# Layer A's output projection as seven half-size block products, with x added by accumulating DMAs and the roundings on ScalarE

## The chip, the cores and the metric

The kernel runs on one core of one Trainium2 chip. The metric is the device time of one execution in microseconds (us). TensorE does the matrix products, VectorE (DVE in the profile) and ScalarE (ACT) work elementwise, GpSimd (POOL) here rounds operands and issues a few DMAs, and SyncE (SP) issues most DMAs. All of them run beside each other and wait for one another through semaphores; each engine works through its own list of instructions in order.

## What is computed

Two layers of a streaming encoder over 1024 frames of width 1024. Layer A (an mLSTM mixer and a pooling mixer) ends with the step that is changed here:

```python
# ya, yb: (1, 1024 tokens, 1024) each;  w_out: (2048, 1024)
return x + jnp.concatenate([ya, yb], axis=-1) @ w_out
```

Layer C (latent attention) begins with `u = rms_norm(x, norm_g) @ w_in` on that result and adds its own output to it at the end, so the result of layer A is needed twice: normalised and transposed at once (`x1h`, `x1l`), and as it is at the end of the kernel (kept in DRAM as `x1_d`).

## The kernel before, in words

All products are float32 products made of three passes in the fast format float32r. Each operand is cut into a rounded part `hi` and the rest `lo = src - hi` (`split`, L156 rounds on GpSimd or L158 on ScalarE, L161 subtracts on VectorE), and `mm3` (L176 to L178) issues hi\*hi, hi\*lo and lo\*hi into the same PSUM bank. A source tile of 128 x 1024 float32 (512 KB) thus costs a DMA, a rounding, a subtraction, and then serves many matmuls of 128 x 128 by 128 x 512.

Up to the projection, layer A's heads are worked through from head 3 to head 0. Their outputs go feature-major to DRAM (`y_d`, 2048 features by 1024 tokens); the last four stores are those of head 0's `zm_pieces` (L336), each behind a block of 24 matmuls (tile `fp_ps`), a SiLU on ScalarE (L415) and a product on VectorE (L417).

The projection then runs over two token halves (512 tokens each), in each over two halves of the output columns, and in each over eight chunks of 256 features. A chunk has 24 matmuls: four token tiles, two row blocks, three passes, into four PSUM banks (tile `o_ps`). So there are 2 x 2 x 8 x 24 = 768 of them. `load_y` reads and splits a chunk of y once per token half (16 tiles, `yh` and `yl`); `load_wo` reads and splits a chunk of the weights for each of the four blocks (32 tiles, `w_hi` and `w_lo`). x itself is loaded into the eight tiles `x1t`, and L875 adds the PSUM banks to it. When four tiles of 128 tokens are complete they are stored to `x1_d` and normalised (`norm_stats`: squares on ScalarE L823, the power on GpSimd L213, the scaling on VectorE L827); `x1_turn` transposes them on TensorE (L834, tile `nt_ps`) into `x1h` and `x1l`. Next come layer C's input products (`u_tiles`, tile `u_ps`), whose first four tiles need the first token half only.

The order in which each engine meets its instructions is settled when the program is built: a scheduler places them by a timeline of its own, within what tile pools (a fixed number of buffers for each tag) and data allow. DMAs that are marked to keep program order, such as the new loads, stay in it on SP.

Of the kernel before, what the change touches and what calls it, by code (L numbers as in the profile page):

```python
# [88 lines left out]
def _hybrid(ctx, tc, nc, ins, consts, out, dbg):  # L89
# [699 lines left out]
    ys = {}

    def load_y(half, n):
        kp = order[n]
        yp = yps[0 if n < EARLY else 1]
        yh = yp.tile([P, 2, HALF], F32R, name="yh", tag=f"yh{n}", bufs=1)
        yl = yp.tile([P, 2, HALF], F32R, name="yl", tag=f"yl{n}", bufs=1)
        wload([P, 2, HALF], y_d[kp * 256:(kp + 1) * 256, half * HALF:(half + 1) * HALF].rearrange("(k p) t -> p k t", p=P), into=(yh, yl))
        ys[half, n] = (yh, yl)
# [6 lines left out]
    load_y(0, 0)
    wo = [load_wo(0, 0)]
    for n in range(1, EARLY):
        load_y(0, n)
# [29 lines left out]
    halves = []  # L837

    def x1_turn(half):
        hs_ = slice(half * HALF, (half + 1) * HALF)  # L840
        norm_turn([t[:] for t in halves[half]], "c_norm_g", lambda k: x1h[:, k, hs_], lambda k: x1l[:, k, hs_])

    for half in range(2):
        if half == 1:
# [4 lines left out]
            x1l = x1p.tile([P, KD, S], F32R, name="x1l")
        x1t = []  # L850
        halves.append(x1t)
        for ch in range(2):
            cs = slice(ch * HALF, (ch + 1) * HALF)
            pss = []
            for j in range(4):
                ps = pmm.tile([P, 512], F32, name="o_ps", tag="mm")
                pss.append(ps)
            for n in range(8):
                if (half, n) not in ys:
                    load_y(half, n)  # L860
# [11 lines left out]
                if half == 0 and ch == 1:  # L872
                    load_y(1, n)
            for j in range(4):
                V.tensor_tensor(x1t[j][:, cs], pss[j][:], x1t[j][:, cs], ALU.add)  # L875
# [510 lines left out]
```

## Time and profile before

| | |
|---|---|
| median of three runs | 1390.33 us (1388.66 to 1391.04) |
| the profiled execution | 1391.1 us, of which the span from first to last instruction is 1389.4 us |
| TensorE clock granted | 0.999 of full speed |
| matmuls of the projection in the trace | 646.85 us to 827.4 us of the span |
| busy share: TensorE, VectorE, ScalarE, GpSimd | 98%, 53%, 34%, 29% |

A profile page has the busy time of each engine, a strip of 40 slices of the span, the DMA queues, the chain of waits that ended last, and the costliest groups of instructions with what they waited for. A matmul's row shows some 0.39 us because a matmul overlaps the next; what one costs on TensorE is the distance from one start to the next. Names such as `w_lo<-w_st,w_hi` are what an instruction writes and reads.

### The profile page before, as it was taken

The page shows a single profiled execution, that of the slowest core. Times are in us where ns is not written, and L with a number is a line of the kernel's source. Part 1 is how long each engine was busy: PE and PEld are TensorE (multiplying, and loading weights), DVE is VectorE, ACT ScalarE, POOL GpSimd, SP SyncE. Part 2 cuts the span into 40 slices and gives each one's busy share as a digit, 9 for nine tenths or more (in the row PEclk, how much of TensorE's full clock was granted, in tenths as well). Part 3 has the DMA queues.
Part 4 walks back from the last instruction along what each step waited for, and adds up shares of the span by engine and source line. Part 5 has one row for each costly group of instructions (what it writes and reads, how often), then busy time and mean ns, then how long its engine had stood idle before and what let it go on. Part 6 is the DMA issues. An engine that isn't in the chain of part 4 may idle for free.

```text
span 1389.4 us, 20100 instructions
## 1 busy us (share of the span) xinstructions
PE 1361.1 (98%) x7724; PEld 1195.2 (86%) x7724; DVE 742.3 (53%) x1600; ACT 470.9 (34%) x1142; POOL 397.5 (29%) x522
## 2 busy tenths in 40 slices
PE   7999999999999999999999999999989999999998
PEld 6878889888988889888888889988889999988887
DVE  6677543653356453743654433631177777778631
ACT  5343233321343132310001112422366666765100
POOL 3137221621134121411532121510244233241310
PEclk9999999999999999999999999999999999999999
DMA  5122312123032212218725241231211211122541
GB/s 200 39 81 69 90 54 62 50 65 99 16 95 65 91 39 61 66 34 313 259 91 167 88 135 45 62 106 46 99 52 36 71 55 62 47 82 73 215 163 50
DMA packets 99231, 124.79 MB, mean 90 GB/s; under 512 B 6103, under 2 KB 70334, under 8 KB 99134
## 3 DMA queue, kind: packets, MB, share of 16 engines
q1 hardware_dynamic: 96398, 113.54, 25.7%
q10 hardware_dynamic: 2736, 9.96, 2.0%
q8 instruction: 61, 1.00, 0.3%
q14 instruction: 36, 0.29, 0.1%
HBM read 98.24 MB, written 25.24 MB: 89 GB/s over the span
## 4 chain that ended last, share of the span: by engine, by line
PE 91%; DVE 3%; ACT 2%; POOL 1%; issue 1%; DMA 1%; SPq 0%; DVEq 0%; ACTq 0%; POOLq 0%
PE fp_ps L176 8%; PE fp_ps L178 8%; PE fp_ps L177 8%; PE s_ps L1194 5%; PE o_ps L177 4%; PE o_ps L176 4%; PE o_ps L178 4%; PE z_ps L178 2%; PE z_ps L177 2%; PE z_ps L176 2%; PE f_ps L176 2%; PE f_ps L178 2%; PE f_ps L177 2%; PE om_ps L176 2%; PE om_ps L178 2%; PE om_ps L177 2%
## 5 line engine op out<-in xcount | busy, mean ns | idle before, releaser
L156 POOL TENSOR_SCALAR w_hi<-w_st 128x1024 fp32r<-128x1024 f32 (+4 forms) x115 | 125.7, 1094 | 549.2 <-PE fp_ps L177 110.8
L161 DVE TENSOR_TENSOR w_lo<-w_st,w_hi 128x1024 fp32r<-128x1024 f32 (+4 forms) x115 | 142.6, 1242 | 168.7 <-POOL w_hi L156 168.4
L176 PE MATMUL fp_ps<-xnh,w_hi 128*128 128x512 f32 x512 | 203.6, 398 | 0.0
L178 PE MATMUL fp_ps<-xnh,w_lo 128*128 128x512 f32 x512 | 202.3, 396 | 0.7 <-DVE w_lo L161 0.7
L177 PE MATMUL fp_ps<-xnl,w_hi 128*128 128x512 f32 x512 | 202.2, 395 | 0.0
L178 PEld LDWEIGHTS fp_ps<-xnh,w_lo 128*128 128x128 f32 x512 | 96.4, 188 | 24.4 <-DVE w_lo L161 1.3
L177 PEld LDWEIGHTS fp_ps<-xnl,w_hi 128*128 128x128 f32 x512 | 96.2, 188 | 21.9
L176 PEld LDWEIGHTS fp_ps<-xnh,w_hi 128*128 128x128 f32 x512 | 96.3, 188 | 21.3
L177 PE MATMUL o_ps<-w_lo,yh 128*128 128x512 f32 x256 | 100.9, 394 | 0.0
L178 PE MATMUL o_ps<-w_hi,yl 128*128 128x512 f32 x256 | 100.4, 392 | 0.0
L176 PE MATMUL o_ps<-w_hi,yh 128*128 128x512 f32 x256 | 99.2, 395 | 0.0
L176 PE MATMUL om_ps<-w_hi,xnh 128*128 128x256 f32 (+1 forms) x256 | 73.3, 287 | 1.0 <-POOL w_hi L156 0.9
L178 PE MATMUL om_ps<-w_hi,xnl 128*128 128x256 f32 (+1 forms) x256 | 73.0, 286 | 0.0
L177 PE MATMUL om_ps<-w_lo,xnh 128*128 128x256 f32 (+1 forms) x256 | 72.7, 285 | 0.1
L1201 ACT ACTIVATE sp<-sp,mx,rq 128x128 f32<-128x128 f32 (+3 forms) x64 | 55.5, 868 | 24.2 <-DVE mx L1200 23.9
L178 PEld LDWEIGHTS o_ps<-w_hi,yl 128*128 128x128 f32 x256 | 48.1, 188 | 11.1
L176 PEld LDWEIGHTS o_ps<-w_hi,yh 128*128 128x128 f32 x256 | 48.1, 188 | 11.0
L177 PEld LDWEIGHTS o_ps<-w_lo,yh 128*128 128x128 f32 x256 | 48.2, 188 | 10.6
L170 DVE TENSOR_TENSOR ptl<-pT_ps,pth 128x512 fp32r<-128x512 f32 (+2 forms) x96 | 51.2, 549 | 6.2 <-ACT pth L169 6.1
L176 PE MATMUL z_ps<-x1h,w_hi 128*128 128x512 f32 x128 | 50.6, 396 | 0.0
L176 PEld LDWEIGHTS om_ps<-w_hi,xnh 128*128 128x128 f32 x256 | 49.1, 192 | 1.8 <-POOL w_hi L156 1.3
L178 PE MATMUL z_ps<-x1h,w_lo 128*128 128x512 f32 x128 | 50.4, 395 | 0.0
(365 smaller groups left out, 3555.4 us busy)
## 6 DMA issues: line engine op xcount, KB each, us to landing
w_st<-in_a_w_in_dram SPq DMA_DIRECT2D x38, 512.0 KB
w_st<-in_a_w_out_dram SPq DMA_DIRECT2D x32, 512.0 KB
w_st<-y_d SPq DMA_DIRECT2D x16, 512.0 KB
rb<-rr_d SPq DMA_DIRECT2D x8, 640.0 KB
x_t<-in_x_dram SPq DMA_DIRECT2D x8, 512.0 KB
y_d<-zp SPq DMA_DIRECT2D x16, 256.0 KB
y_d<-xc SPq DMA_DIRECT2D x16, 256.0 KB
x1t<-in_x_dram SPq DMA_DIRECT2D x8, 512.0 KB
```

Of the source, the lines that this page charges most:

```text
L156: i = G.tensor_scalar(hi, src, 1.0, 1.0, ALU.mult, ALU.mult)
L161: return i, V.tensor_tensor(lo, src, hi.bitcast(F32), ALU.subtract)
L170: V.tensor_tensor(lo, src, hi.bitcast(F32), ALU.subtract)
L176: T.matmul(acc, lh, rh, start=start and i == 0, stop=False)
L177: T.matmul(acc, lh, rl, start=False, stop=False)
L178: T.matmul(acc, ll, rh, start=False, stop=stop and i == n - 1)
L1194: T.matmul(ps[:, 0:w], l[:, js], r_[:, cs], start=i == 0, stop=i == 4)
L1201: A.activation(sp[:, 0:n], sp[:, 0:n], AF.Exp, bias=mx[:, 2:3], scale=rq[:, jt:jt + 1], accum_out=mx[:, 3:4])
```

## The change

The projection is one product of two-by-two blocks: y by token half (row 1 is the second 512 tokens, row 2 the first) and by feature half, the weights by feature half and column half. The change computes it by the Strassen-Winograd scheme: seven products of half-size blocks in place of eight, with sums and differences of blocks formed ahead (S1, S2 from y; T1, T2 from the weights) and of results formed after. With A for y and B for the weights the seven are, by number n: 0: A11 B11; 1: (A11-A21)(B22-B12); 2: S1 T1 with S1 = A21+A22, T1 = B12-B11; 3: S2 T2 with S2 = S1-A11, T2 = B22-T1; 4: A22 (T2-B21); 5: A12 B21; 6: (A12-S2) B22.

Each product covers 512 tokens, 1024 features (four chunks `c` of 256) and 512 columns, so it has 4 x 24 = 96 matmuls, 672 in all. All tokens go through at once: nothing of the result is complete before product 4 (first token half) and product 6 (second half). Every operand is rounded by ScalarE (`split(..., "act")`), 56 of them; the 32 block sums are VectorE operations on 128 x 1024 (`sums`, and the line with `y12`). `evict` takes the products out of PSUM: 0, 1 and 2 by ScalarE copies, the others by VectorE with the sums of the results. x is no longer loaded into `x1t` ahead: after product 3, `G.dma_start(..., accum_op=ALU.add)` issues eight DMAs from GpSimd's queue that add x to the tiles in SBUF. The normalisation of the first four tiles stands after product 4, that of the others is done tile by tile in product 6, which goes bank by bank.

```diff
-    for half in range(2):
...
-        for ch in range(2):
...
-            for n in range(8):
-                if (half, n) not in ys:
-                    load_y(half, n)
-                yh, yl = ys[half, n]
-                wh, wl = wo.pop(0) if wo else load_wo(n, ch)
...
-                for j in range(4):
-                    js = slice(j * P, (j + 1) * P)
-                    mm3(pss[j][:], [((yh[:, k, js], yl[:, k, js]), (wh[:, k, :], wl[:, k, :])) for k in range(2)],
-                        start=n == 0, stop=n == 7)
...
-            for j in range(4):
-                V.tensor_tensor(x1t[j][:, cs], pss[j][:], x1t[j][:, cs], ALU.add)
-            if half == 1 and ch == 0:
-                x1_turn(0)
+    def fetch(pl, tag, bufs, src, n=2 * HALF):
+        st = pl.tile([P, n], F32, name="o_" + tag, tag=tag, bufs=bufs)
+        tc.keep_in_program_order(SY.dma_start(st[:, 0:2 * HALF].rearrange("p (k n) -> p k n", n=HALF), src))
+        return st[:, 0:2 * HALF]
+    def operand(pl, tags, bufs, src, n=2 * HALF):
...
+        split(hi[:, 0:2 * HALF], lo[:, 0:2 * HALF], src, "act")
...
+    def banks(n):
+        kinds = [(pmm, "mm")] * 4 if n % 2 == 0 else [(pmm, "mm")] + [(ptr, "tr")] * 3
...
+    def load(n, c):
...
+        if n == 1:
+            S2[c] = fetch(sp, "s2", NC, y_src(1, 1, c))
+            T2[c] = fetch(tp_, "t2", NC, w_src(2, 2, c))
+            T1[c] = fetch(tp_, "t1", NC, w_src(1, 2, c))
+            S1[c] = fetch(tp_, "s1", NC, y_src(1, 2, c))
+        elif n == 2:
+            raw[n, c] = stage(y_src(2, 2, c)), stage(w_src(1, 1, c))
...
+    def sums(n, c):
...
+        if n == 1:
+            a_, b_ = raw[n, c] = tmp(), tmp()
+            tt(a_, S2[c], S1[c], ALU.subtract)
+            tt(b_, T2[c], T1[c], ALU.subtract)
...
+    def evict(n, j, ps):
+        r1, r2 = x1t[4 + j], x1t[j]
+        if n == 0:
+            A.copy(r1[:, L], ps)
...
+        elif n == 3:
+            tt(r1[:, R], ps, r1[:, L], ALU.add)
+            tt(r2[:, L], r1[:, R], r2[:, L], ALU.add)
+            tt(r1[:, R], r1[:, R], r2[:, R], ALU.add)
+            tt(r2[:, R], r2[:, L], r2[:, R], ALU.add)
+            for t, jj in ((r2, j), (r1, 4 + j)):
+                G.dma_start(t[:], x_in[jj * P:(jj + 1) * P, :], accum_op=ALU.add)
+        elif n == 4:
+            tt(r2[:, L], r2[:, L], ps, ALU.subtract)
...
+    AHEAD, SUM, FAR = 2, 3, 6
...
+    for i, (n, c) in enumerate(steps):
...
+        chunk_mm(pss[n], *ops.pop((n, c)), c)
...
+        if n == 5:
+            y12 = stage(y_src(2, 1, c))
+            tt(S2[c], y12, S2[c], ALU.subtract)
+            last.append(operand(lp, ("b_hi", "b_lo"), NC, stage(w_src(2, 2, c))))
...
+    x1_turn(0)
+    pl = banks(6)
+    for j in range(4):
+        for c in range(NC):
+            chunk_mm(pl, *last[c], c, (j,))
+        evict(6, j, pl[j][:])
+        x1_done(4 + j)
+        norm_stats(op, [x1t[4 + j][:]])
```

The engines' own lists show three places. The first is SP before the change, at the last four stores of head 0 (`y_d<-xc`); `w_st` are staging tiles of the chunks, `x1t` the tiles that get x.

```order
L866 DMA x1t_6663<-in_x_dram 128x1024 [waits DMAHW6_49]
L191 DMA w_st_5771<-y_d_66 128x2x512 [waits DMAHW7_49,DVE_49]
L866 DMA x1t_6695<-in_x_dram 128x1024 [waits DMAHW0_49,Activation_49]
L866 DMA x1t_6727<-in_x_dram 128x1024 [waits DMAHW1_49]
L336 DMA y_d_66<-xc_4630 128x512 [waits DMAHW2_49,DVE_49]
L336 DMA y_d_66<-xc_4649 128x512 [waits DMAHW3_49,DVE_49]
L202 DMA w_st_5833<-in_a_w_out_dram 128x2x512 [waits DMAHW5_49,DMAHW4_49,DVE_49]
L202 DMA w_st_6505<-in_a_w_out_dram 128x2x512 [waits DMAHW7_49,DVE_49]
L336 DMA y_d_66<-xc_4630 128x512 [waits DMAHW6_49,DVE_49]
L202 DMA w_st_6535<-in_a_w_out_dram 128x2x512 [waits DMAHW4_49,DVE_49]
L336 DMA y_d_66<-xc_4649 128x512 [waits DMAHW0_49,DVE_49]
L202 DMA w_st_5957<-in_a_w_out_dram 128x2x512 [waits DMAHW1_49,Activation_49]
```

The same place on SP after the change; `o_x1t` are the raw tiles of product 0, the `s2`, `t2`, `t1` and `s1` tiles the blocks that product 1 takes differences of.

```order
L804 DMA o_x1t_5761<-in_a_w_out_dram 128x2x512 [waits DMAHW5_49]
L804 DMA o_x1t_5763<-y_d_66 128x2x512 [waits DMAHW6_49,Activation_49]
L804 DMA o_x1t_5765<-in_a_w_out_dram 128x2x512 [waits DMAHW7_49]
L336 DMA y_d_66<-xc_4630 128x512 [waits DMAHW0_49,DVE_49]
L336 DMA y_d_66<-xc_4649 128x512 [waits DMAHW1_49,DVE_49]
L336 DMA y_d_66<-xc_4630 128x512 [waits DMAHW2_49,DVE_49]
L336 DMA y_d_66<-xc_4649 128x512 [waits DMAHW3_49,DVE_49]
L804 DMA o_s2_5923<-y_d_66 128x2x512 [waits DMAHW4_49,Activation_49]
L804 DMA o_t2_5925<-in_a_w_out_dram 128x2x512 [waits DMAHW5_49,PE_49]
L804 DMA o_t1_5927<-in_a_w_out_dram 128x2x512 [waits DMAHW6_49]
L804 DMA o_s1_5929<-y_d_66 128x2x512 [waits DMAHW7_49]
L804 DMA o_s2_5931<-y_d_66 128x2x512 [waits DMAHW0_49,Activation_49]
```

All eight loads of product 0 stand ahead of the four stores, and all 16 loads of product 1 behind the last of them, followed by those of product 2.

The second place is VectorE while the operands of the early blocks are made. Before, each row is the rest of one operand that GpSimd has rounded.

```order
L161 TENSOR_TENSOR w_lo_6031<-w_st_6029,w_hi_6030 128x1024 [waits DMAHW5_49,Pool_49]
L161 TENSOR_TENSOR yl_6062<-w_st_6063,yh_6061 128x1024 [waits DMAHW6_49,Pool_49]
L161 TENSOR_TENSOR w_lo_6069<-w_st_6067,w_hi_6068 128x1024 [waits DMAHW7_49,Pool_49]
L161 TENSOR_TENSOR yl_6100<-w_st_6101,yh_6099 128x1024 [waits DMAHW0_49,Pool_49]
L161 TENSOR_TENSOR w_lo_6107<-w_st_6105,w_hi_6106 128x1024 [waits DMAHW1_49,Pool_49]
```

After, the sums for three products stand between the operands of products 1 (`6154`, `6158`) and 2 (from `6188`).

```order
L840 TENSOR_TENSOR o_s1_5929<-o_s1_5929,o_st_6019 128x1024 [waits DMAHW4_49]
L161 TENSOR_TENSOR a_lo_6154<-o_tmp_6107,a_hi_6153 128x1024 [waits PE_49,Activation_49]
L840 TENSOR_TENSOR o_t1_5927<-o_t1_5927,o_st_6021 128x1024 [waits DMAHW5_49]
L161 TENSOR_TENSOR w_lo_6158<-o_tmp_6108,w_hi_6157 128x1024 [waits Activation_49]
L840 TENSOR_TENSOR o_s2_5923<-o_s1_5929,o_s2_5923 128x1024 [waits DVE_49]
L840 TENSOR_TENSOR o_s1_5937<-o_s1_5937,o_st_6059 128x1024 [waits DMAHW6_49]
L161 TENSOR_TENSOR a_lo_6188<-o_s1_5929,a_hi_6187 128x1024 [waits PE_49,Activation_49]
L840 TENSOR_TENSOR o_t1_5935<-o_t1_5935,o_st_6061 128x1024 [waits DMAHW7_49]
L840 TENSOR_TENSOR o_t2_5925<-o_t2_5925,o_t1_5927 128x1024 [waits DVE_49]
L161 TENSOR_TENSOR w_lo_6192<-o_t1_5927,w_hi_6191 128x1024 [waits Activation_49]
```

Counted from the first sum (`o_tmp_5987`) to the rest of the weights of product 2's second chunk (`w_lo_6226`), VectorE's list has 32 rows of 128 x 1024 there.

The third place is VectorE at the end of the second block before the change, where the first token half is completed in PSUM (L875), and the operands of the next block follow.

```order
L161 TENSOR_TENSOR yl_6430<-w_st_6431,yh_6429 128x1024 [waits DMAHW1_49,PE_49,Pool_49]
L875 TENSOR_TENSOR x1t_6035<-o_ps_6179,x1t_6035 128x512 [waits PE_49]
L161 TENSOR_TENSOR w_lo_6537<-w_st_6535,w_hi_6536 128x1024 [waits Pool_49]
L875 TENSOR_TENSOR x1t_6073<-o_ps_6180,x1t_6073 128x512 [waits PE_49]
L875 TENSOR_TENSOR x1t_6111<-o_ps_6181,x1t_6111 128x512 [waits PE_49]
```

After, the first token half is completed at the end of product 4; `DMASW` are the semaphores of the accumulating DMAs, and `w_lo_6700` and `w_lo_6756` belong to product 5's second and third chunk.

```order
L161 TENSOR_TENSOR a_lo_6752<-o_st_6586,a_hi_6751 128x1024 [waits DMAHW0_49,PE_49,Activation_49]
L840 TENSOR_TENSOR x1t_5915<-x1t_5915,o_ps_6599 128x512 [waits DMASW2_49,PE_49]
L161 TENSOR_TENSOR w_lo_6700<-o_st_6527,w_hi_6699 128x1024 [waits DMAHW7_49,Activation_49]
L840 TENSOR_TENSOR x1t_5916<-x1t_5916,o_ps_6600 128x512 [waits DMASW4_49,PE_49]
L840 TENSOR_TENSOR x1t_5917<-x1t_5917,o_ps_6601 128x512 [waits DMASW6_49,DVE_49,PE_49]
L840 TENSOR_TENSOR x1t_5918<-x1t_5918,o_ps_6602 128x512 [waits DMASW7_49,DVE_49,PE_49]
L840 TENSOR_TENSOR o_s2_5923<-o_st_6791,o_s2_5923 128x1024 [waits DMAHW4_49]
L161 TENSOR_TENSOR a_lo_6801<-o_st_6627,a_hi_6800 128x1024 [waits DMAHW2_49,Activation_49]
L161 TENSOR_TENSOR w_lo_6756<-o_st_6588,w_hi_6755 128x1024 [waits DMAHW1_49,Activation_49]
```

The four additions now wait for the accumulating DMAs as well as for TensorE, and operands of product 5 stand behind them in the list.

More of the change, by code (lines that the diff above doesn't have):

```diff
@@ L785, in _hybrid @@
     op = octx.enter_context(pool("aout", side="right"))
-    yctx = ExitStack()
-    yps = [yctx.enter_context(pool("ain", side="right"))]
+    actx = ExitStack()
+    aop = actx.enter_context(pool("aops", side="right"))
     order = [v for h in reversed(range(M_HEADS)) for v in (4 + h, h)]
[L789 to L797, printed above, removed]
@@ new lines, in a_op, with b_op, early @@
+    def a_op(src):
+        return operand(aop, ("a_hi", "a_lo"), AB, src)
+    def b_op(src):
+        wp, WN, nst, nsp = wpool["now"]
+        return operand(wp, ("w_hi", "w_lo"), nsp, src, WN)
+    def early(src):
+        wp, WN, nst, nsp = wpool["now"]
+        return fetch(wp, "w_st", nst, src, WN)
+    L, R = slice(0, HALF), slice(HALF, D)
+    def banks(n):
+        kinds = [(pmm, "mm")] * 4 if n % 2 == 0 else [(pmm, "mm")] + [(ptr, "tr")] * 3
+        return [bank.tile([P, 512], F32, name="o_ps", tag=tag) for bank, tag in kinds]
@@ L803, in _hybrid, with chunk_mm, tt @@
+    def chunk_mm(pss, ao, bo, c, js=range(4)):
+        for j in js:
+            sl = slice(j * P, (j + 1) * P)
+            mm3(pss[j][:], [((ao[0][:, k, sl], ao[1][:, k, sl]), (bo[0][:, k, :], bo[1][:, k, :])) for k in range(2)],
+                start=c == 0, stop=c == NC - 1)
+    def tt(o, a_, b_, op_):
+        V.tensor_tensor(o, a_, b_, op_)
     wz = [feat_w(A_ZM + f * P) for f in range(2)]
[L804 to L807, printed above, removed]
+    ops, raw = {}, {}
@@ L815, in _hybrid, with stage, tmp @@
     sctx = ExitStack()
-    wpool["stage"] = (sctx.enter_context(pool("stage")), STAGE)
+    sp = sctx.enter_context(pool("sums"))
+    tctx = ExitStack()
+    tp_ = tctx.enter_context(pool("sums_b"))
+    x1t = [op.tile([P, D], F32, name="x1t", tag="x1t", bufs=8) for _ in range(NT)]
+    S1, S2, T1, T2 = {}, {}, {}, {}
+    ST, TMP = 6, 3
+    def stage(src):
+        return fetch(sp, "st", ST, src)
+    def tmp():
+        return sp.tile([P, 2 * HALF], F32, name="o_tmp", tag="tmp", bufs=4)[:]
@@ new lines, in load @@
+    def load(n, c):
+        if (n, c) in ops:
+            return
+        if n == 1:
[6 more added lines that the diff above has]
+        elif n == 4:
+            raw[n, c] = stage(y_src(2, 2, c)), stage(w_src(2, 1, c))
+        elif n == 5:
+            raw[n, c] = stage(y_src(2, 1, c)), stage(w_src(2, 1, c))
@@ L884, in _hybrid, with x1_done @@
-    yctx.close()
+        norm_turn([t[:] for t in x1t[4 * half:4 * half + 4]], "c_norm_g", lambda k: x1h[:, k, hs_], lambda k: x1l[:, k, hs_])
+    def x1_done(j):
+        SY.dma_start(x1_d[j * P:(j + 1) * P, :], x1t[j][:])
+        if dbg and "x1" in dbg:
+            SY.dma_start(dbg["x1"][j * P:(j + 1) * P, :], x1t[j][:])
+    steps = [(n, c) for n in range(6) for c in range(NC)]
+    AHEAD, SUM, FAR = 2, 3, 6
+    loaded = summed = prepped = 0
+    pss = {}
+    lctx = ExitStack()
+    last = []
@@ new lines, in _hybrid @@
+    last = [(a_op(S2[c]), b_) for c, b_ in enumerate(last)]
+    sctx.close()
+    x1n_ctx = ExitStack()
+    x1p = x1n_ctx.enter_context(pool("x1n"))
+    x1h = x1p.tile([P, KD, S], F32R, name="x1h")
+    x1l = x1p.tile([P, KD, S], F32R, name="x1l")
+    x1_turn(0)
[6 more added lines that the diff above has]
+        norm_stats(op, [x1t[4 + j][:]])
+    lctx.close()
+    actx.close()
```

105 lines of the change are left out of this document (70 added, 35 removed).

## The prediction

> **What bounds the kernel now.** I read the page first: the busy times, then the chain of waits.
>
> ```profile
> span 1389.4 us, 20100 instructions
> ...
> PE 1361.1 (98%) x7724; PEld 1195.2 (86%) x7724; DVE 742.3 (53%) x1600; ACT 470.9 (34%) x1142; POOL 397.5 (29%) x522
> ...
> PE 91%; DVE 3%; ACT 2%; POOL 1%; issue 1%; DMA 1%; SPq 0%; DVEq 0%; ACTq 0%; POOLq 0%
> ```
>
> TensorE is busy for 98% of the span and 91% of the chain that ended last lies on it. To see whether this holds in the projection, I asked for the groups by shape between 560 and 860 us.
>
> ```profile
> L177 PE MATMUL o_ps<-w_lo,yh 128*128 128x512 f32 x256 | 100.9, 394 | 0.0
> L161 DVE TENSOR_TENSOR w_lo<-w_st,w_hi 128x1024 fp32r<-128x1024 f32 x36 | 48.1, 1337 | 72.1 <-POOL w_hi L156 72.1
> L156 POOL TENSOR_SCALAR w_hi<-w_st 128x1024 fp32r<-128x1024 f32 x36 | 41.8, 1162 | 93.9 <-PE o_ps L178 65.5 <-DMA w_st<-in_a_w_out_dram 15.6 <-PE fp_ps L177 6.9
> L161 DVE TENSOR_TENSOR yl<-w_st,yh 128x1024 fp32r<-128x1024 f32 x16 | 29.5, 1844 | 23.6 <-POOL yh L156 23.6
> L823 ACT ACTIVATE nt_sq<-x1t 128x1024 f32<-128x1024 f32 x8 | 8.5, 1061 | 116.1 <-DVE x1t L875 115.4 <-ACT nt_sq L823 0.6
> ```
>
> The matmuls have no idle time ahead of them (the last column), while GpSimd waits 65.5 us for TensorE to release buffers: the operands are ready early. So TensorE sets the pace, and matmuls taken out here are time taken out, as long as the operands stay ahead. What one costs is read in the timeline of TensorE, at the stage's start, at the turn of the first token half, and at its end.
>
> ```profile
> 646.85 0.39 PE L176 MATMUL o_ps<-w_hi,yh 128*128 128x512 f32 x1
> 647.08 0.40 PE L177 MATMUL o_ps<-w_lo,yh 128*128 128x512 f32 x1
> ...
> 779.81 1.47 PE L834 MATMUL nt_ps<-ident,x1t 128*128 128x128 f32 x12
> 781.04 0.48 PE L176 MATMUL o_ps<-w_hi,yh 128*128 128x512 f32 x1
> ...
> 827.40 0.39 PE L178 MATMUL o_ps<-w_hi,yl 128*128 128x512 f32 x1
> 827.62 0.33 PE L176 MATMUL u_ps<-w_hi,x1h 128*128 128x352 f32 x1
> ```
>
> The projection runs from 646.85 to 827.62, 180.8 us. In it are 768 matmuls and 32 transposes; twelve of the latter take 781.04 - 779.81 = 1.23 us, so all take about 3.5. That leaves 177.3 us, 0.231 us a matmul. I count with this, not with the 0.39 us of a row.
>
> **What goes.** One product of eight, 96 matmuls: 96 x 0.231 = 22.2 us. The 32 transposes stay and lie between matmuls as before. This is the whole gain: nothing else in the stage is on the path. The profiled execution took 1391.1 us, so without any new wait it would be 1368.9 us; the median of the three runs is 0.8 us under the profiled one, hence 1368.1 us. A product takes 96 x 0.231 = 22.2 us, a chunk 5.5 us, and product n begins at 646.85 + 22.2 n if nothing waits. The rest is what could make it wait.
>
> **VectorE.** Before, 48 subtractions of 128 x 1024; after, 56 of them and 32 block sums, while the 16 additions of x go. How long they take depends on GpSimd, as these rows of the two engines show.
>
> ```profile
> 621.91 1.23 DVE L161 TENSOR_TENSOR w_lo<-w_st,w_hi 128x1024 fp32r<-128x1024 f32 x1 [2.13 <-POOL w_hi L156]
> 623.05 1.49 DVE L408 SCALAR_TENSOR_TENSOR zp<-pool_ps,cols,zp 128x512 f32<-128x512 f32 x2
> ...
> 663.39 2.05 DVE L161 TENSOR_TENSOR yl<-w_st,yh 128x1024 fp32r<-128x1024 f32 x1
> ...
> 688.05 1.28 DVE L875 TENSOR_TENSOR x1t<-o_ps,x1t 128x512 f32<-128x512 f32 x2
> ...
> 664.35 2.00 POOL L156 TENSOR_SCALAR yh<-w_st 128x1024 fp32r<-128x1024 f32 x1
> ```
>
> Alone such a row takes 1.23 us, and the next starts 1.14 us after it; beside a rounding on GpSimd both take 2.0. With the roundings on ScalarE the second case goes, so I take 1.14 to 1.23 for the 88 rows: 100 to 108 us. The evictions add 28 rows of 128 x 512 at 0.64 (half of 1.28), 18 us. Over some 155 us this fits, but not evenly: products 1 to 3 all draw their sums from blocks that arrive at the same time. The tightest place is product 2's second chunk, whose weights (`w_lo_6226`) stand 32 rows of 128 x 1024 behind the first sum. When can that sum begin? Its four loads stand on SP behind the last store of y:
>
> ```profile
> 649.24 0.34 SPq L336 DMA_DIRECT2D y_d<-xc  x1
> ...
> 653.60 0.37 SPq L191 DMA_DIRECT2D w_st<-y_d  x1
> ...
> 658.17 1.04 POOL L156 TENSOR_SCALAR yh<-w_st 128x1024 fp32r<-128x1024 f32 x1 [1.74 <-DMA w_st<-y_d]
> ...
> 653.00:658.00 5.00, 5.00 (x23) 4.00 (x23) 1.22 (x1) 0.00 (x0) 1.06 (x1) 1.00 0.87 277
> 663.00:668.00 5.00, 5.00 (x23) 4.13 (x22) 5.00 (x4) 0.00 (x0) 5.00 (x3) 1.00 1.05 388
> ```
>
> That store went out at 649.24. A load beside others takes 4.6 us from its issue to the wait that it ends (653.60 to 658.17), and full queues move 388 GB/s, so four loads of 0.52 MB take 5.4 us and their fixed part: the first sum begins at about 658. The 32 rows take 36.5 us at 1.14 and 39.4 at 1.23, and about three times VectorE waits for a rounding on ScalarE, some 1.06 us by the square's row of the same shape: 697.7 to 700.6. TensorE wants the result after 2 x 96 + 24 + 4 matmuls, at 646.85 + 220 x 0.231 = 697.7. So it waits 0 to 2.9 us; were the loads late by 2 us, up to 5. I take 2 us. Behind that the list is lighter, four or five rows a chunk of 5.5 us, and it keeps up. Products 0 and 1 are covered: product 0's eight loads are issued ahead of the last stores, as x was before, and product 1 needs its first chunk at 669, ten us after the blocks.
>
> [...]
>
> **ScalarE** gets 56 roundings of 1.06 us and twelve copies out of PSUM, about 67 us in 155, and stands at 0.00 of 5 us in the 388 GB/s window; what hides it is that it works two chunks ahead, and its cost without that is in the term above. **GpSimd** loses the roundings and only issues. **SP** issues as many loads as before: 56 of 512 KB against 48 and 8 of x.
>
> **The accumulating DMAs.** Nothing in this trace is a DMA that adds; the page's queues are hardware queues and instruction fetches.
>
> ```profile
> q1 hardware_dynamic: 96398, 113.54, 25.7%
> q10 hardware_dynamic: 2736, 9.96, 2.0%
> ...
> q14 instruction: 36, 0.29, 0.1%
> ```
>
> The bound from below is a load of the same size at 388 GB/s, 4.2 MB in 10.8 us; below nothing it can't go, since x waits for nothing today. From above I take twice that, since the destination is read as well; it is also near the slowest queue shown, q14's 0.29 MB in 0.1% of the span, 209 GB/s. The eight are issued when product 3 leaves PSUM: its first bank is complete near 733, the first addition chain near 738, and the last, by 16 evictions and 5 operand rows on VectorE (16 x 0.64 + 5 x 1.14 = 16 us), near 749. They are needed by the additions at the end of product 4, and behind these on VectorE stand one sum and two rests up to `w_lo_6756`, four rows or 4.1 us, which TensorE wants in product 5's third chunk, at 646.85 + 532 x 0.231 + 2 = 771.7. So all eight must have landed by about 767. From 738 that is 29 us, in which seven loads of 0.52 MB run too. At the price of a load: 4.2 + 3.7 = 7.9 MB, 20 us and 2 of latency, landed by 760, no wait. At twice: 12.1 MB, 31 us and 2, landed at 771, 4 us late, and product 6, whose operands then come late too, loses some 3 more. I take 2 us, nearer to the cheap end, because a load and a store of the same row is the nearest thing shown, with both ends kept.
>
> [...] The trace shows VectorE's two-input rows and GpSimd's at 2.0 us where they meet. If issuing a DMA on GpSimd were slowed so too, the eight issues, at the 1.05 of a GpSimd row, would take 16 in place of 8 us, and the last landing would move from 760 to some 765: still in time at the cheap price. [...]
>
> **The last product** goes bank by bank, so its four chunks are all wanted within 5.5 us of its start at 646.85 + 133 + 4. Their 12 rows of sums and rests lie in product 5's 22 us beside the normalisation. I put 1 us on it, 0 to 3. What follows is covered: the first four `u_ps` tiles need only the first token half.
>
> **Sum.** 1391.1 - 22.2 + 2 + 2 + 1 = 1373.9 for the profiled execution, less 0.8 for the median: 1373.1 us. The likeliest case's own range goes from no wait, 1368.1, to all three at their far ends, 1368.1 + 5 + 7 + 3 = 1383.
>
> **Rivals.** *The accumulating DMAs block VectorE* (slower). The additions stand in order ahead of product 5's operands, so every us that the eighth lands after 767 is a us of TensorE. The gain is gone when that is 20 us, at 787: the eight then run at about 4.2 MB in 47 us, 90 GB/s. If an added byte cost as much as four loaded ones, 16.8 + 3.7 MB take 53 us and 2, landing at 793: 26 us of waiting, and with the other terms 5 us more, 1368.1 + 31 = 1399. For it: no row shows the price, and the waits stand where nothing can pass. Against it: at 388 GB/s the loads of that time fill only a third of it, and one more read explains a price of two, not of four. I give 9% to slower than 1393, 5% to within 0.2%, 6% to a price of about three, 16 us late, 1368.1 + 16 + 3 = 1387.
>
> *The loads and VectorE set the pace in products 1 and 2.* If the stream of 24 loads moved at the 277 GB/s of a window that wasn't full, 12.6 MB would take 45.5 us, 13 more than at 388; the sums would come as late, and product 2 begins with its slack of a few us used up: about 10 us of waits, 1368.1 + 10 + 3 = 1381. For it: 24 loads queue at once, and VectorE's 32 rows leave no gap. Against it: where the queue was full (a DMA share of 1.05), the window shows 388. I give 12%.
>
> *The change doesn't do what it says*, the matmuls go and something else fills the time, would show in `u_ps` waiting for the second half's normalisation; four tiles (96 matmuls) lie over that chain. If they hid nothing of it, one tile's addition, square, power and scaling would show, four rows of about the square's 1.06 us, and the time would be 1377. I give it 2%.
>
> **How the numbers follow.** The forecast has 66%. A measurement of this kernel can tell 0.2%, 2.8 us, from no change, so faster means under 1387.5. Faster: 66 + 12 + 2 + 6 = 86%, within 5%, slower 9%. The range takes the likeliest case from its floor, the late loads, and the lower part of the slow accumulation: 1368 to 1386, leaving out some 18%.
>
> **What would show it.** Right: the `o_ps` matmuls from about 646.9 to 806 to 812, 672 in number, 0.231 us apart; VectorE's 1024-wide rows at 1.14 to 1.23; a wait of TensorE of a few us near 698, released by VectorE's `w_lo`. The accumulating DMAs' landing is read at the additions to `x1t` near 760: if they wait for a DMA past 767, TensorE waits near 772. Wrong: waits of TensorE in products 0, 1 or 3, waits of VectorE for the loads beyond 658, or matmuls further apart.

## The result, and the profile after

| | before | after |
|---|---|---|
| median, beside each other on one chip | 1389.49 us (4 runs, 1388.47 to 1391.04) | 1378.57 us (4 runs, 1378.19 to 1379.60) |
| ratio | | 0.9922 (95% interval 0.9904 to 0.9939) |
| profiled execution, its span | 1391.1, 1389.4 us | 1378.2, 1376.5 us |
| first `o_ps` to first `u_ps` matmul | 646.85 to 827.62, 180.8 us | 647.05 to 816.57, 169.5 us |

The kernel is faster by 0.8%, inside the range, 5.5 us above the predicted 1373.1. The profiled executions differ by 12.9 us and the medians by 10.9, since the one before was the slowest of its four and the one after the fastest. The projection became 11.3 us shorter, not the 17.2 that the prediction leaves after its three terms of waiting. The page of the changed kernel has one queue that was not there before, and much less of the chain on TensorE:

```profile
span 1376.5 us, 20009 instructions
...
PE 1340.7 (97%) x7628; PEld 1176.6 (85%) x7628; DVE 782.9 (57%) x1655; ACT 533.4 (39%) x1210; POOL 352.5 (26%) x485
...
q0 software_dynamic: 1152, 4.19, 1.6%
...
PE 83%; DVE 6%; issue 4%; DMA 3%; ACT 2%; POOL 2%; SPq 1%; DVEq 0%; POOLq 0%; ACTq 0%
```

The new queue is that of the accumulating DMAs: 4.19 MB in 1.6% of the 16 engines' span, 22 us of all of them, 190 GB/s. That is the price of the prediction's far end, twice a load, not the price it took. What TensorE made of it stands in its timeline (start, duration, and in brackets what it waited for):

```profile
647.05 0.39 PE L176 MATMUL o_ps<-w_hi,a_hi 128*128 128x512 f32 x1
...
699.46 0.50 PE L177 MATMUL o_ps<-w_lo,a_hi 128*128 128x512 f32 x1 [1.32 <-DVE w_lo L161]
...
774.92 0.80 PE L177 MATMUL o_ps<-w_lo,a_hi 128*128 128x512 f32 x1 [3.66 <-DVE w_lo L161]
...
780.57 0.40 PE L178 MATMUL o_ps<-w_hi,a_lo 128*128 128x512 f32 x1
...
793.45 0.51 PE L178 MATMUL o_ps<-b_hi,a_lo 128*128 128x512 f32 x1 [1.43 <-DVE a_lo L161]
...
800.09 0.49 PE L178 MATMUL o_ps<-b_hi,a_lo 128*128 128x512 f32 x1 [0.57 <-DVE a_lo L161]
...
816.57 0.32 PE L176 MATMUL u_ps<-w_hi,x1h 128*128 128x352 f32 x1
```

Four waits, 7.0 us together. And between 774.92 and 780.57 lie 13 distances from one matmul to the next, 5.65 us, where 13 x 0.231 = 3.0: 2.65 us more are lost without any wait. The windows show why; the third number from the right is the granted clock.

```profile
773.50:773.60 0.10, 0.00 (x0) 0.00 (x0) 0.10 (x1) 0.10 (x1) 0.00 (x0) 1.00 1.15 471
773.60:773.70 0.10, 0.00 (x0) 0.00 (x0) 0.10 (x2) 0.10 (x1) 0.00 (x0) 0.76 0.95 389
780.40:780.50 0.10, 0.10 (x2) 0.10 (x1) 0.09 (x1) 0.00 (x0) 0.10 (x1) 0.61 1.26 492
780.50:780.60 0.10, 0.10 (x2) 0.06 (x2) 0.10 (x1) 0.00 (x0) 0.10 (x1) 1.00 1.24 369
```

From 773.65 to 780.48, 6.8 us, TensorE had half its clock: 0.50 was granted, and its matmuls stood 0.43 us apart in place of 0.231. VectorE's timeline names what the long wait is made of:

```profile
659.13 1.23 DVE L840 TENSOR_TENSOR o_tmp<-o_s,o_s 128x1024 f32<-128x1024 f32 x1 [3.98 <-DMA o_s<-y_d]
...
698.19 1.22 DVE L161 TENSOR_TENSOR w_lo<-o_t,w_hi 128x1024 fp32r<-128x1024 f32 x1
...
760.96 0.69 DVE L840 TENSOR_TENSOR x1t<-x1t,o_ps 128x512 f32<-128x512 f32 x1 [2.74 <-DMA x1t<-in_x_dram]
...
767.50 0.69 DVE L840 TENSOR_TENSOR x1t<-x1t,o_ps 128x512 f32<-128x512 f32 x1 [5.85 <-DMA x1t<-in_x_dram]
770.77 0.69 DVE L840 TENSOR_TENSOR x1t<-x1t,o_ps 128x512 f32<-128x512 f32 x1 [2.58 <-DMA x1t<-in_x_dram]
...
773.65 1.22 DVE L161 TENSOR_TENSOR w_lo<-o_st,w_hi 128x1024 fp32r<-128x1024 f32 x1
```

The last addition of product 4 starts at 770.77, held by an accumulating DMA; behind it come one sum, one rest, and then the rest that TensorE waits for. Meanwhile the DMA engines are full (a share above 1) and yet move less than in the window of 388 GB/s before:

```profile
755.00:760.00 5.00, 5.00 (x24) 4.10 (x23) 2.96 (x3) 2.34 (x4) 0.00 (x0) 1.00 1.05 245
```

### The profile page after: what moved, and what is told of

It is laid out like the page before. It is cut to its first block, busy times and chain, and to the rows that moved or that the text cites. A ratio compares the mean times of both kernels' runs of the same rounds, so it can differ in the third digit from the quotient of the medians.

```text
span 1376.5 us, 20009 instructions
## 1 busy us (share of the span) xinstructions
PE 1340.7 (97%) x7628; PEld 1176.6 (85%) x7628; DVE 782.9 (57%) x1655; ACT 533.4 (39%) x1210; POOL 352.5 (26%) x485
## 3 DMA queue, kind: packets, MB, share of 16 engines
q0 software_dynamic: 1152, 4.19, 1.6%
## 4 chain that ended last, share of the span: by engine, by line
PE 83%; DVE 6%; issue 4%; DMA 3%; ACT 2%; POOL 2%; SPq 1%; DVEq 0%; POOLq 0%; ACTq 0%
PE fp_ps L176 8%; PE fp_ps L178 8%; PE fp_ps L177 8%; PE s_ps L1321 5%; PE z_ps L178 2%; PE z_ps L177 2%; PE z_ps L176 2%; PE f_ps L176 2%; PE f_ps L178 2%; PE f_ps L177 2%; PE om_ps L176 2%; PE om_ps L178 2%; PE om_ps L177 2%; PE pT_ps L1347 2%; PE q_ps L176 2%
## 5 line engine op out<-in xcount | busy, mean ns | idle before, releaser
L156 POOL TENSOR_SCALAR w_hi<-w_st 128x1024 fp32r<-128x1024 f32 (+4 forms) x83 | 89.7, 1082 | 457.0 <-PE fp_ps L177 108.6
L161 DVE TENSOR_TENSOR w_lo<-w_st,w_hi 128x1024 fp32r<-128x1024 f32 (+4 forms) x83 | 100.2, 1211 | 95.4 <-POOL w_hi L156 95.1
L178 PEld LDWEIGHTS fp_ps<-xnh,w_lo 128*128 128x128 f32 x512 | 96.4, 188 | 24.5 <-DVE w_lo L161 1.4
L177 PE MATMUL o_ps<-w_lo,a_hi 128*128 128x512 f32 x192 | 76.8, 400 | 5.0 <-DVE w_lo L161 5.0
L178 PE MATMUL o_ps<-w_hi,a_lo 128*128 128x512 f32 x192 | 76.8, 400 | 0.0
L176 PE MATMUL o_ps<-w_hi,a_hi 128*128 128x512 f32 x192 | 72.4, 398 | 0.0
L1328 ACT ACTIVATE sp<-sp,mx,rq 128x128 f32<-128x128 f32 (+3 forms) x64 | 55.5, 868 | 22.3 <-DVE mx L1327 22.2
L169 ACT CAST pth<-pT_ps 128x512 fp32r<-128x512 f32 (+2 forms) x96 | 43.3, 478 | 21.7 <-PE pT_ps L1347 19.3
L177 PE MATMUL z_ps<-x1l,w_hi 128*128 128x512 f32 x128 | 50.3, 393 | 0.0
L1347 PE MATMUL pT_ps<-ident,sp 128*128 128x128 f32 x288 | 43.9, 276 | 5.8 <-DVE sp L1330 2.1
```

The source lines that it names most:

```text
L156: i = G.tensor_scalar(hi, src, 1.0, 1.0, ALU.mult, ALU.mult)
L161: return i, V.tensor_tensor(lo, src, hi.bitcast(F32), ALU.subtract)
L169: A.copy(hi, src)
L176: T.matmul(acc, lh, rh, start=start and i == 0, stop=False)
L177: T.matmul(acc, lh, rl, start=False, stop=False)
L178: T.matmul(acc, ll, rh, start=False, stop=stop and i == n - 1)
```

## Theories

**Theory 1:** what is lost after 760 us comes from the accumulating DMAs. They cost the engines twice a load's time, and VectorE, which works in order, stands still behind what they hold back. **Theory 2:** VectorE has too many rows by then, whatever it waits for. **Theory 3:** the ordinary loads of product 5's operands are late. Each experiment was run several times, with the kernel before on the same chip; ratios are to that kernel, so the changed kernel's 0.9922 is the mark. The stage is the time from the first `o_ps` to the first `u_ps` matmul in the profiled execution: 169.5 us for the changed kernel, and 180.8 - 22.2 = 158.6 if nothing waited.

## Experiments: is it the accumulating DMAs?

**Without them.** x is not added.

```diff
-            for t, jj in ((r2, j), (r1, 4 + j)):
-                G.dma_start(t[:], x_in[jj * P:(jj + 1) * P, :], accum_op=ALU.add)
```

> The eight accumulating DMAs are left out, so x is not added; every row of VectorE, ScalarE and TensorE stays. Theory 1 (the additions of product 4 wait in VectorE's order for accumulating DMAs that move at about half a load's rate, TensorE then waits 3.8 us for a rest behind them and runs 13 matmuls at half clock, 2.7 us): both go, and of the 2.3 us in product 6 a part: 1378.6 - 6.5 - (0 to 2.3) = 1370 to 1372 us, no TensorE wait over 1 us near 772 and no stretch at half clock there. Theory 2 (VectorE has simply too many rows by product 5, whatever it waits for): unchanged, 1378 us, the wait near 775 still there. Theory 3 (the ordinary loads of product 5's operands come late, because they share the DMA engines): 1370 to 1374 too, but the wait would then be put down to a load of o_st; the kernels with the accumulating DMAs kept tell it from theory 1.

1369.97 us, ratio 0.9852 (0.9835 to 0.9870), stage 160.3. Of all the waits of TensorE in the stage one is left, that of product 2:

```profile
PE o_ps L177 <- DVE w_lo L161: 1.2, 1, 1.2
```

Theory 2 falls: every row of VectorE was still there. Some 9 us hang on eight DMAs.

**The same DMAs without the add.** Each overwrites its tile with x.

```diff
-                G.dma_start(t[:], x_in[jj * P:(jj + 1) * P, :], accum_op=ALU.add)
+                G.dma_start(t[:], x_in[jj * P:(jj + 1) * P, :])
```

> The same eight DMAs on the same GpSimd queue at the same place, but without the add: each overwrites its tile with x (the block sums are lost), so VectorE's order and all waits stay as they are and only the price of the add goes. Theory 1 with the price in the add: the eight land by about 760 as 4.2 MB at 388 GB/s, the additions don't wait, 1370 to 1373 us. Theory 1 with the price in the queue (descriptors made by software, whatever they do): landings to 770 as now, 1377 to 1380 us. Theory 2: 1378 us with the additions on time and TensorE still waiting near 775.

1369.55 us, ratio 0.9841 (0.9826 to 0.9855). The queue's share of the window from 735 to 780 us and the time from issue to landing, first of the changed kernel, then of this one:

```profile
q0 software_dynamic: 1152, 4.19, 48.1%
...
x1t<-in_x_dram POOLq DMA_DIRECT2D x8, 512.0 KB, 13.7
```

```profile
q0 software_dynamic: 1152, 4.19, 24.5%
...
x1t<-in_x_dram POOLq DMA_DIRECT2D x8, 512.0 KB, 6.2
```

The same packets, bytes, queue and place: 48.1% of 45 us are 21.6 us of all engines, 24.5% are 11.0. The add doubles the price, almost exactly (a factor of 1.96); the software queue costs nothing of its own that shows here, since without the add it moves 381 GB/s, against the 388 of the loads before. That a read of the destination is the reason, as the prediction took it, isn't shown here.

## Experiments: which wait of VectorE?

**The first half's four ahead.** The additions of product 4 need only the tiles of the first token half; the other four are issued behind.

```diff
-            for t, jj in ((r2, j), (r1, 4 + j)):
-                G.dma_start(t[:], x_in[jj * P:(jj + 1) * P, :], accum_op=ALU.add)
+            for t, jj in ((r2, j),):
+                tc.keep_in_program_order(G.dma_start(t[:], x_in[jj * P:(jj + 1) * P, :], accum_op=ALU.add))
...
+            if n == 3:
+                for j in range(4, 8):
+                    tc.keep_in_program_order(G.dma_start(x1t[j][:], x_in[j * P:(j + 1) * P, :], accum_op=ALU.add))
```

> All eight accumulating DMAs stay, but those of the first token half, which the additions of product 4 wait for, are issued ahead of the four of the second half. Theory 1: the four land after half of the bytes, by about 760, the additions don't wait past 765, TensorE's wait at 775 and the half clock behind it go: 1378.6 - 6.5 = 1372 us, 1370 to 1373. Theory 2: unchanged, 1378 us. Theory 3: the same bytes move in the same time, so operand loads are as late as before, 1377 to 1379 us.

1372.27 us, ratio 0.9860 (0.9847 to 0.9873), as theory 1 had it. But VectorE still stood still, now for something else, and TensorE still waited a little (VectorE's timeline, then TensorE's):

```profile
757.63 1.28 DVE L840 TENSOR_TENSOR x1t<-x1t,o_ps 128x512 f32<-128x512 f32 x2
767.75 1.23 DVE L840 TENSOR_TENSOR o_s<-o_st,o_s 128x1024 f32<-128x1024 f32 x1 [8.84 <-DMA o_st<-y_d]
...
770.63 1.22 DVE L161 TENSOR_TENSOR w_lo<-o_st,w_hi 128x1024 fp32r<-128x1024 f32 x1
```

```profile
771.90 0.50 PE L177 MATMUL o_ps<-w_lo,a_hi 128*128 128x512 f32 x1 [1.15 <-DVE w_lo L161]
```

The row that waits 8.84 us is the first block sum for the last product, which began only near 783. Its plain load, the thirteenth of 16 from `y_d`, went out at 751.54 (SP's timeline) and landed at 767.73, after 16 us; in the run without the accumulating DMAs the same load took 5.6 (751.81 to 757.38).

```profile
751.54 0.36 SPq L804 DMA_DIRECT2D o_st<-y_d  x1
```

**The additions behind the rest.** The DMAs as in the changed kernel, the four additions behind product 5's third chunk on VectorE. The stores and the normalisation of these tiles move with them.

```diff
+        if (n, c) == (5, 0):
+            for j in range(4):
+                r2 = x1t[j]
+                tc.keep_in_program_order(V.tensor_tensor(r2[:, L], r2[:, L], pss[4][j][:], ALU.subtract))
+            for j in range(4):
+                x1_done(j)
+            norm_stats(op, [t[:] for t in x1t[0:4]])
...
-            for j in range(4):
-                evict(n, j, pss[n][j][:])
-            if n == 4:
+            if n != 4:
                 for j in range(4):
-                    x1_done(j)
-                norm_stats(op, [t[:] for t in x1t[0:4]])
+                    evict(n, j, pss[n][j][:])
```

> The DMAs stay as they are; the four additions of product 4 are put behind the rest for product 5's third chunk on VectorE (they stood four rows ahead of it). Theory 1: TensorE's wait at 775 goes with its half clock; product 5's fourth chunk, whose rest stands six rows behind the additions (771 + 7 = 778 against 777 wanted), may wait 1 us: 1372 to 1374 us. Theory 2: the same number of rows, so it only moves the wait by a chunk: 1377 to 1379 us. Theory 3: 1377 to 1379 us, with that rest itself waiting for its load.

1377.60 us, ratio 0.9905 (0.9889 to 0.9920): within its interval no better than the changed kernel, though no addition stands in the way any more. Behind the wait shown came four more, 3.3 us together. VectorE's and TensorE's rows:

```profile
756.10 1.22 DVE L161 TENSOR_TENSOR w_lo<-o_st,w_hi 128x1024 fp32r<-128x1024 f32 x1
769.67 1.23 DVE L840 TENSOR_TENSOR o_s<-o_st,o_s 128x1024 f32<-128x1024 f32 x1 [12.36 <-DMA o_st<-y_d]
...
771.95 2.08 DVE L161 TENSOR_TENSOR w_lo<-o_st,w_hi 128x1024 fp32r<-128x1024 f32 x1
```

```profile
774.09 0.51 PE L177 MATMUL o_ps<-w_lo,a_hi 128*128 128x512 f32 x1 [3.13 <-DVE w_lo L161]
```

So theory 1 as I held it was half of it, and theory 3 has a part in it. Two waits lie side by side on VectorE, one for the accumulating DMAs (to 770.8) and one for a plain load that shares the engines with them (to 769.7). Who removes one finds the other.

**Only that block sum behind.** The reverse: additions as in the changed kernel, the last product's sums behind product 5's rests.

```diff
-            tt(S2[c], y12, S2[c], ALU.subtract)
+            tc.keep_in_program_order(V.tensor_tensor(S2[c], y12, S2[c], ALU.subtract))
```

> The four accumulating DMAs of each half and the additions stay where they are; only the block sums for the last product, which the run with deferred additions showed waiting 12.4 us for a plain load, are put behind product 5's rests on VectorE. Theory 1a (two waits lie side by side on VectorE, the additions' for the accumulating DMAs to 770.8 and the sum's for a plain load slowed by them to 769.7; taking one away leaves the other): the additions still end at about 771.4, the rest for the third chunk follows 1 to 2 us earlier than now, 1376 to 1378 us, TensorE's wait near 773 still 2 to 3 us. Theory 1b (the plain load is the one that counts): the wait goes, 1372 us.

1376.90 us, ratio 0.9915 (0.9901 to 0.9928): theory 1a. The last addition starts at 771.08 in place of 770.77, with the rests right behind the additions; TensorE still waited 2.78 us, and 2.87 more at 782.74:

```profile
771.08 0.69 DVE L840 TENSOR_TENSOR x1t<-x1t,o_ps 128x512 f32<-128x512 f32 x1 [2.55 <-DMA x1t<-in_x_dram]
771.69 1.22 DVE L161 TENSOR_TENSOR a_lo<-o_st,a_hi 128x1024 fp32r<-128x1024 f32 x1
772.82 1.22 DVE L161 TENSOR_TENSOR w_lo<-o_st,w_hi 128x1024 fp32r<-128x1024 f32 x1
```

**Both.** The edits of the run with the first half ahead and of the last one.

> Both at once: the accumulating DMAs of the first token half go first, and the last product's sums are behind product 5's rests. Theory 1a: nothing on VectorE waits past 762 ahead of the rest for the third chunk, so TensorE's 1.15 us at 772 go, and of the 1.1 us near 786 to 789 what came from the late sums: 1372.3 - (1.1 to 2.2) = 1370 to 1371 us, as without the DMAs at all. Theory 1b: the same as with the order of the DMAs alone, 1372 us, since there the load is the only wait that was left.

1373.71 us, ratio 0.9897 (0.9884 to 0.9911): a miss, no better than the DMAs' order alone. The wait at 772 did go. But the last product's second weights came late instead, with a new stretch at half clock (785.97 to 789.38). SP, ScalarE and TensorE:

```profile
762.40 4.62 SPq L804 DMA_DIRECT2D o_st<-in_a_w_out_dram  x1
```

```profile
783.64 1.04 ACT L158 CAST b_hi<-o_st 128x1024 fp32r<-128x1024 f32 x1 [3.60 <-DMA o_st<-in_a_w_out_dram]
```

```profile
784.74 0.50 PE L176 MATMUL o_ps<-b_hi,a_hi 128*128 128x512 f32 x1 [1.64 <-ACT b_hi L158]
...
786.00 0.79 PE L177 MATMUL o_ps<-b_lo,a_hi 128*128 128x512 f32 x1 [0.76 <-DVE b_lo L161]
```

That load left SP between 762.4 and 767.0, behind all four stores of the first half's tiles, and landed at 783.6. With the DMAs' order alone it left later, at 769.0, behind three of them, and landed earlier, at 779.9. So it isn't lateness in going out; what held it so long stays open.

**Product 3's sums behind, too.** The edits before, and product 3's eight sums behind product 2's rests.

```diff
-            tt(S2[c], S1[c], S2[c], ALU.subtract)
-            tt(T2[c], T2[c], T1[c], ALU.subtract)
+            tc.keep_in_program_order(V.tensor_tensor(S2[c], S1[c], S2[c], ALU.subtract))
+            tc.keep_in_program_order(V.tensor_tensor(T2[c], T2[c], T1[c], ALU.subtract))
```

> As the run before, and in addition product 3's eight block sums stand behind product 2's rests on VectorE (three of them stood ahead of the rest for product 2's second chunk, 3 x 1.14 us). If that wait is VectorE's number of rows, as the prediction had it: TensorE's 1.1 to 1.3 us at 699 go, 1369 to 1370 us, and the stage is then within 1 to 2 us of 160 - 3.5 = 157 + 0.2 for 672 matmuls and 32 transposes. If it is the first loads' lateness alone: unchanged, 1370 to 1371 us.

1372.64 us, ratio 0.9888 (0.9875 to 0.9902), above the 1369 to 1370 expected, since the last product's weights were late here as well. In the stage the edit did what it was for: 164.0 us against 165.3 in the run before, and TensorE's wait at 699 (1.15 us there) is gone. So that wait was VectorE's list (four of the eight sums stood ahead of the rest that TensorE waited for, not three), and its order could be mended.

**More of it.** x is added twice to the second half: twelve accumulating DMAs.

```diff
-            for t, jj in ((r2, j), (r1, 4 + j)):
+            for t, jj in ((r1, 4 + j), (r2, j), (r1, 4 + j)):
```

> The changed kernel with x added twice to the second half: twelve accumulating DMAs in place of eight, two of the added ones in the queue ahead of the first half's last. Theory 1: 2 x 0.52 MB at about 190 GB/s is 5.5 us, so TensorE's wait near 775 grows from 3.7 to between 7 and 9 us; the half clock behind it stays some 5 us long (it doesn't grow with the wait), so 1378.6 + (3 to 6) = 1382 to 1385 us. If the clock's loss grows with the wait: 1385 to 1388 us. Theory 2 (VectorE's number of rows): unchanged, 1378 us.

1380.15 us, ratio 0.9937 (0.9924 to 0.9951). The wait grew to 7.37 us, as theory 1 had it; the time grew by 1.6 us, where 3 to 6 were expected.

```profile
778.78 0.79 PE L177 MATMUL o_ps<-w_lo,a_hi 128*128 128x512 f32 x1 [7.37 <-DVE w_lo L161]
```

```profile
775.00:775.10 0.10, 0.00 (x0) 0.00 (x0) 0.10 (x1) 0.10 (x1) 0.00 (x0) 0.53 0.86 246
781.80:781.90 0.10, 0.10 (x2) 0.05 (x2) 0.10 (x1) 0.09 (x1) 0.10 (x1) 0.83 1.20 266
```

The half clock again lasted 6.8 us (775.0 to 781.83), but more than half of that lay in the wait itself, so it cost (781.83 - 778.78) / 2 = 1.5 us in place of 2.65; and the waits of product 6, 2.0 us in the changed kernel, were covered by the longer one before them. So the stage grew by 0.5 us only (170.05): 3.7 more of the wait, less some 1.1 and 2.0.

## Experiments: a version that keeps x and not the waits

**The second half's x after product 5.** Its four DMAs were meant to meet idle engines; product 3's sums stay behind.

```diff
-            for t, jj in ((r2, j), (r1, 4 + j)):
-                G.dma_start(t[:], x_in[jj * P:(jj + 1) * P, :], accum_op=ALU.add)
+            G.dma_start(r2[:], x_in[j * P:(j + 1) * P, :], accum_op=ALU.add)
...
             tt(r1[:, L], ps, r1[:, L], ALU.add)
+            G.dma_start(r1[:], x_in[(4 + j) * P:(5 + j) * P, :], accum_op=ALU.add)
```

> The first half's accumulating DMAs stay after product 3; each of the second half's four is issued after that tile's addition of product 5, where the runs so far show the DMA engines at 0 to 0.5 of their time; product 3's sums stand behind product 2's rests. If the rest of the loss is the accumulating DMAs' traffic against the loads of products 5 and 6 (theory 1, second part): the loads of 755 to 775 move at 350 GB/s or more, TensorE's waits at 772 and between 784 and 789 go, and the half clock with them: 1369 to 1370 us, as without these DMAs. If the loads are late for want of buffers or of places on SP's queue: the waits near 785 stay, 1372 us. Should the last product's additions wait for the late DMAs, TensorE isn't held, since only the second half's normalisation hangs on them.

1375.20 us, ratio 0.9890 (0.9876 to 0.9904): a miss. TensorE waited neither at 699 nor at 772. But VectorE stood still at another place, for the store of a finished tile (the scaling overwrites the tile, so it has to wait for the store). That store, the first of the second half's, took 9.9 us beside the accumulating DMAs; in the changed kernel it took 2.7. The rests `x1l` of the first half, which TensorE's transposes need out of PSUM, stood behind. Half clock followed from 805.1 to 808.5:

```profile
803.77 0.75 DVE L943 TENSOR_SCALAR x1t<-x1t,nt_rs 128x1024 f32<-128x1024 f32 x1 [7.02 <-DMA x_d<-x1t]
```

```profile
805.30 1.97 PE L950 MATMUL nt_ps<-ident,x1t 128*128 128x128 f32 x8 [3.30 <-DVE x1l L166]
```

**The second half's x after product 6.** The same with the line in the last branch.

```diff
             tt(r1[:, R], ps, r1[:, R], ALU.add)
+            G.dma_start(r1[:], x_in[(4 + j) * P:(5 + j) * P, :], accum_op=ALU.add)
```

> As the run before, but the second half's four are issued after the additions of the last product. The same 1369 to 1370 us if the normalisation of the second half, some 6 us later for each tile, is still covered by the first four u_ps tiles (96 matmuls, some 18 us); 3 to 5 us more, 1372 to 1375 us, if it isn't.

1369.55 us, ratio 0.9849 (0.9836 to 0.9861): as fast as without the DMAs at all, and faster than both kernels; its interval lies wholly below the changed kernel's. Some 1.3 us of this are the place of product 3's sums (164.0 against 165.3 above). The stage is 160.7 us with one wait left in it. The window shows 364 GB/s where the changed kernel had 245, and the transposes of the second half, behind the first four `u_ps` tiles, waited 0.73 us:

```profile
790.66 0.50 PE L178 MATMUL o_ps<-b_hi,a_lo 128*128 128x512 f32 x1 [0.80 <-DVE a_lo L161]
```

```profile
755.00:765.00 10.00, 10.00 (x45) 8.14 (x44) 6.27 (x8) 6.19 (x9) 0.00 (x0) 1.00 1.04 364
```

## Experiment: the roundings

**Roundings back on GpSimd.** The other part of the change undone, the seven products kept.

```diff
-        split(hi[:, 0:2 * HALF], lo[:, 0:2 * HALF], src, "act")
+        split(hi[:, 0:2 * HALF], lo[:, 0:2 * HALF], src, "pool")
```

> The changed kernel with its 56 roundings on GpSimd in place of ScalarE, the other part of the change undone. By the prediction's step on VectorE, a 128x1024 row beside a rounding on GpSimd takes 2.0 in place of 1.14 us: of the 32 rows ahead of product 2's second chunk some 12 to 14 lie beside one, 10 to 12 us more, so TensorE waits 10 us or more near 698, partly given back to what waits at 775; 1385 to 1395 us, the gain mostly gone. If VectorE isn't slowed by roundings of this kernel: 1377 to 1380 us.

1394.14 us, ratio 1.0029 (1.0017 to 1.0040): the whole gain and a little more is gone. VectorE's rest takes 2.05 us where it starts beside a rounding of GpSimd (first fence VectorE, second GpSimd), and the two longest waits of TensorE stand in product 2, where the prediction had the tightest place:

```profile
693.71 2.05 DVE L161 TENSOR_TENSOR w_lo<-o_t,w_hi 128x1024 fp32r<-128x1024 f32 x1
```

```profile
692.89 1.80 POOL L156 TENSOR_SCALAR w_hi<-o_t 128x1024 fp32r<-128x1024 f32 x1 [1.31 <-DVE o_t L840]
```

```profile
695.82 0.78 PE L177 MATMUL o_ps<-w_lo,a_hi 128*128 128x512 f32 x1 [2.65 <-DVE w_lo L161]
...
708.27 0.80 PE L177 MATMUL o_ps<-w_lo,a_hi 128*128 128x512 f32 x1 [5.04 <-DVE w_lo L161]
```

Ten waits of TensorE in the stage make 16.4 us, and four stretches at half clock, 17.1 us long, lie beside them; the stage took 185.4 us. So the seven products bring nothing here without the move of the roundings; that move without the seven products wasn't tried.

## Why the prediction was right, and where it was not

**What goes: right.** Matmuls outside the waits stand 0.231 us apart as before, and where the waits are taken out the stage is 160.3 or 160.7 us against the 158.6 of the sum. Less what still waited there (1.2 and 0.8), 0.5 to 1.3 us are left over; I haven't traced them.

**VectorE: right in place and size.** Taken as 2 us, it was 1.32, at 699.46, released by the named rest. The first sum began at 659.1 instead of 658. Its cause is shown by the run that moved product 3's sums: the wait went. That ScalarE hides the rounding, and GpSimd could not, is shown by the last experiment; how much of it is VectorE's slower rows, and how much GpSimd's own list, it doesn't part.

**The accumulating DMAs: the right mechanism, the wrong size.** The step that failed is "I take 2 us, nearer to the cheap end, because a load and a store of the same row is the nearest thing shown". The far end of that bound was the true one: twice a load's price, last addition at 770.8 against the 771 worked out there. The wait was 3.66 us against "4 us late". To this came two things that the prediction did not have. The half clock behind the wait took 2.65 us more. And the same traffic slowed the plain loads (16 us for one that takes 5.6 without it), so that a block sum without any hurry became as late as the additions; in the changed kernel this second wait was hidden behind the first, and it decided what each remedy was worth. The term was 6.3 us, not 2. The 2 us of latency in the sums of that step were an estimate, which no run shows alone; shown are 5.6 us from issue to landing for that plain load in the run without the accumulating DMAs.

**GpSimd's issuing: right.** The eight issues went out from 739.6 to 751.5 in the changed kernel, where 738 to 749 was expected; an issue took 1.11 us in the mean, not the 2.0 of two rows that meet, beside a VectorE that was busy for 12.3 of the 12.4 us from 739.6 to 752, with two-input rows:

```profile
L925 POOL DMA_DIRECT2D x1t<-in_x_dram x8 | 7.2, 1108 | 122.2 <-DVE x1t L840 119.6 <-issue 1.7 <-ACT w_hi L158 0.9
```

**The last product: too small by half.** Taken as 1 us, it was 1.43 + 0.57 = 2.0. The run without the DMAs has none of it, so it belongs to the term above, as the prediction's own sentence on the far end had it ("product 6 ... loses some 3 more").

**The sum.** Stage: 158.6 + 1.32 + 6.3 + 2.0 = 168.2, measured 169.5; the 1.3 us left over are of the size of those above. The part behind the stage came out 1.9 us shorter (1389.4 - 827.6 = 561.8, after 1376.5 - 816.6 = 559.9); it lies between 559.9 and 563.6 in the runs here, and I make nothing of it. But it helped: the stage was 5.9 us longer than the prediction's 180.8 - 17.2 = 163.6, the profiled execution only 4.3 longer than its 1373.9. That much of the closeness is luck.

**The rivals.** That the accumulating DMAs would block VectorE was the right place; its price of four loads was wrong by a factor of two. The loads of products 1 and 2 did not set the pace, and `u_ps` waited for nothing.

## What to carry to other kernels

A DMA that adds cost as much as two here (21.6 us of all engines against 11.0): count it twice against the engines' time, and ask which plain loads and stores share these us with it. On an engine that works in order, look at every row ahead of the urgent one and not only at the one that waits now: when a wait is removed, the next one may stand in its shadow, as it did in the two runs here that moved one of two rows. Put such traffic where the engines are idle and nothing in order hangs on it: half of it after product 6, with product 3's sums moved as well, gave back all of the 9 us.
